# Group softmax over 285 MB: VectorE and ScalarE run hardware loops of 12 rows with semaphores of their own

## The chip, the cores and the metric

One core of a Trainium2 chip. The time is the device time of one execution in microseconds (us). The profile is one execution taken by the hardware profiler; its span, from the first to the last instruction, is about 2 us shorter than the time.

## The reference, cut to what matters

```python
B, N, D, G = 4, 4096, 4352, 8            # x: float32
x_g = x.reshape(B, N, G, D // G)         # groups of 544
x_g = x_g - x_g.max(axis=-1, keepdims=True)
exp = np.exp(x_g)
out = exp / exp.sum(axis=-1, keepdims=True)
```

285.21 MB are read and as much is written; each element is reduced, exponentiated and scaled once.

## The kernel before

A buffer holds 128 partitions of two rows (4.46 MB). SyncE (SP) issues 64 loads and 64 stores. For each row VectorE (DVE) takes the eight maxima, ScalarE (ACT) does eight exponentials that also sum, and VectorE multiplies eight times by the reciprocal. Everything is unrolled in Python, and a framework puts in the waits.

```python
pool = ctx.enter_context(tc.tile_pool(name="io", bufs=NBUF))       # NBUF = 6, R = 2
...
def expo(i, r):
    nc.vector.reduce_max(out=mx, in_=xr, axis=mybir.AxisListType.X, negate=True)
    for g in range(G):
        nc.scalar.activation(out=xr[:, g, :], in_=xr[:, g, :], func=Exp,
                             bias=mx[:, g:g + 1], scale=1.0, accum_out=sm[:, g:g + 1])

def scale(i, r):
    nc.vector.reciprocal(out=rs, in_=sums.pop((i, r)))
    for g in range(G):
        nc.vector.tensor_scalar_mul(out=xr[:, g, :], in0=xr[:, g, :], scalar1=rs[:, g:g + 1])
...
for n in range(len(work) + 1):           # work: 128 rows of 128 partitions
    if n < len(work):
        expo(*work[n])
    if n:
        i, r = work[n - 1]
        scale(i, r)
        if r == spans[i][1] - 1:
            store(i)
            if i + AHEAD < nt:           # AHEAD = 5
                load(i + AHEAD)
```

(Cuts are marked with "...", names shortened.)

## Time and profile before

| | before |
|---|---|
| time, median of the first 3 runs (lowest to highest) | 1335.78 us (1335.38 to 1341.09) |
| time and span of the profiled run | 1335.33 and 1333.5 us |
| first DMA issued, last part of the last store landed | 0.73 and 1332.6 us |
| instruction packets while the kernel ran | 28 |

The chain that ended last, followed back from the last instruction, by engine and then by line:

```profile
DMA 92%; DVE 4%; ACT 1%; SPq 1%; issue 0%; DVEq 0%; ACTq 0%
```

92% of the chain is data movement. The page's share of DMA is a mean over 16 DMA engines, though, and the last store lands over a stretch of 12.2 us (1320.4 to 1332.6), 0.9 us before the end: the kernel ends with the slowest of the 16. I call one DMA engine's work a **lane**. In the trace each transfer lands in 16 parts (2048 landing records for 128 transfers); the **lag** of a lane is how much later its part lands than the earliest part of the same transfer.

### The profile page before, as it was taken

Reading aid. Unit: us, or ns where it says so; the run is one execution under the profiler, and the core shown is the slowest. Engines: PE = TensorE matmul, PEld = TensorE weight load, DVE = VectorE, ACT = ScalarE, POOL = GpSimd, SP = SyncE. Lnnn points to the kernel's source line nnn. Section 1 sums busy time; section 2 is a strip of 40 time slices with the busy share of each in tenths; the row PEclk is TensorE's granted clock in tenths of the full one; section 3 lists DMA queues with packets and bytes.
Section 4 is the critical chain, followed back from the end, with each engine's and each line's share of the span. In section 5 each row is a group of like instructions: output and inputs, shape, how many; then the busy total and the mean of one; then the engine's idle time right before and its main releaser. Section 6 shows DMA issues by size and latency. Waiting matters only on the chain.

```text
span 1333.5 us, 3809 instructions
## 1 busy us (share of the span) xinstructions
DVE 1041.7 (78%) x1280; ACT 764.4 (57%) x2049; POOL 0.2 (0%) x4
## 2 busy tenths in 40 slices
DVE  5999887787877878778778787787877878778771
ACT  4777665555655556555565565655656556555560
POOL 0000000000000000000000000000000000000000
DMA  9999999999999999999999999999999999999996
GB/s 403 428 423 432 432 432 431 433 432 431 432 432 434 434 432 434 430 434 434 434 431 433 434 434 434 431 432 435 432 434 432 431 434 434 433 435 433 433 433 283
DMA packets 18460, 570.66 MB, mean 428 GB/s; under 512 B 2048, under 2 KB 2048, under 8 KB 2048
## 3 DMA queue, kind: packets, MB, share of 16 engines
q1 hardware_dynamic: 18432, 570.43, 99.3%
q14 instruction: 28, 0.23, 0.0%
HBM read 285.21 MB, written 285.21 MB: 428 GB/s over the span
## 4 chain that ended last, share of the span: by engine, by line
DMA 92%; DVE 4%; ACT 1%; SPq 1%; issue 0%; DVEq 0%; ACTq 0%
DMA out_dram<-xt 89%; DMA xt<-in_x_dram 3%; DVE mx L58 2%; DVE xt L76 1%; ACT xt L62 1%; SPq L47 1%; DVE rs L74 0%; DVEq L121 0%; ACTq L121 0%; ACTq L62 0%; SPq L50 0%
## 5 line engine op out<-in xcount | busy, mean ns | idle before, releaser
L62 ACT ACTIVATE xt<-xt,mx 128x544 f32<-128x544 f32 x1024 | 751.3, 735 | 522.0 <-DVE mx L58 504.4
L58 DVE TENSOR_REDUCE mx<-xt 128x8 f32<-128x4352 f32 x128 | 599.3, 4683 | 253.5 <-DMA xt<-in_x_dram 253.5
L76 DVE TENSOR_SCALAR xt<-xt,rs 128x544 f32<-128x544 f32 x1024 | 434.3, 499 | 4.5
L62 ACT ACTIVATION_READ_ACCUMULATOR xt<-xt,mx 128x1 f32 x1024 | 191.4, 187 | 0.0
L74 DVE RECIPROCAL rs<-sm 128x8 f32<-128x8 f32 x128 | 24.9, 194 | 4.0 <-ACT xt L62 4.0
L62 ACT ACT_TABLE_LOAD x1 | 1.3, 1283 | 13.7 <-DMA xt<-in_x_dram 13.7
L110 POOL MEMSET const-bfloat16-1.0<- 128x1 bf16 x1 | 0.1, 101 | 0.0
L110 POOL MEMSET const-uint8-127<- 128x1 uint8 x1 | 0.1, 101 | 0.0
L110 POOL MEMSET const-float32-0.0<- 128x1 f32 x1 | 0.1, 98 | 0.2 <-issue 0.2
L110 POOL MEMSET const-float32-1.0<- 128x1 f32 x1 | 0.1, 98 | 0.0
## 6 DMA issues: line engine op xcount, KB each, us to landing
xt<-in_x_dram SPq DMA_DIRECT2D x64, 4352.0 KB, 30.8
out_dram<-xt SPq DMA_DIRECT2D x64, 4352.0 KB, 40.7
```

Of the source, the lines that this page charges most:

```text
L47: nc.sync.dma_start(out=xt[:, :spans[i][1] * D], in_=rows(xf, i))
L58: nc.vector.reduce_max(out=mx, in_=xr, axis=mybir.AxisListType.X, negate=True)
L62: nc.scalar.activation(out=xr[:, g, :], in_=xr[:, g, :], func=mybir.ActivationFunctionType.Exp, bias=mx[:, g:g + 1], scale=1.0, accum_out= ...
L74: nc.vector.reciprocal(out=rs, in_=sums.pop((i, r)))
L76: nc.vector.tensor_scalar_mul(out=xr[:, g, :], in0=xr[:, g, :], scalar1=rs[:, g:g + 1])
L110: nc = _bacc.Bacc("TRN2", target_bir_lowering=False, num_devices=1)
```

## The change

Intent: keep the same work and the same DMAs, but let VectorE and ScalarE run a short loop in place of an unrolled stream. Buffers are fixed, so a loop body covers the 12 rows of the six buffers. A wait compares with a constant and counts the semaphore down at once, so that each turn finds the same values.

```diff
-    pool = ctx.enter_context(tc.tile_pool(name="io", bufs=NBUF))
+    ctx.enter_context(tc.tile_critical(no_gpsimd_drain=True))
+    ctx.enter_context(nc.cleanup_on_exit())
+    bufs = [ctx.enter_context(nc.sbuf_tensor(f"xt{b}", [P, R * D], f32)) for b in range(NT)]
+    landed = [nc.alloc_semaphore(f"landed{b}") for b in range(NT)]
+    stored = [nc.alloc_semaphore(f"stored{b}") for b in range(NT)]
...
+    def vector_max(s):
+        if s % R == 0:
+            nc.vector.sem_inc(landed[s // R], -16).wait_op(landed[s // R], 16, "sem-ge")
+        nc.vector.reduce_max(out=mx[:, s, :], in_=row(s), axis=X, negate=True).then_inc(max_done, 1)
+    def vector_scale(s):
+        nc.vector.sem_inc(exp_done, -1).wait_op(exp_done, 1, "sem-ge")
+        nc.vector.reciprocal(out=rs[:, s, :], in_=sm[:, s, :]).then_inc(rec_done, 1)
+        nc.vector.sem_inc(rec_done, -1).wait_op(rec_done, 1, "sem-ge")
...
+    def loop(engine):
+        return nc.Fori(
+            0, turns, engines=OrderedEngineSet([engine.engine]), head_slot={engine.engine: 0})
...
+        def _(vector):
+            vector_max(0)
+            with loop(vector):                          # S = 12 rows, turns = 10
+                for s in range(S):
+                    vector_max((s + 1) % S)
+                    vector_scale(s)
+            for n in range(turns * S, nr):              # the last 8 rows
+                if n + 1 < nr:
+                    vector_max((n + 1) % S)
+                vector_scale(n % S)
...
+        def _(scalar):
+            scalar.preload_act_table(Exp)
+            with loop(scalar):
+                for s in range(S):
+                    scalar_exp(s)
+            for n in range(turns * S, nr):
+                scalar_exp(n % S)
```

SyncE's part stays unrolled: five loads ahead, then for each buffer a wait for its two scaled rows, the store, a wait for the store of the buffer that comes free, and the next load.

## The prediction

> **What bounds the kernel now.** I read the page's busy shares first, then its DMA lines, the waits, one steady stretch of VectorE's timeline, and last the stages at the end of the run.

> ```profile
> DVE 1041.7 (78%) x1280; ACT 764.4 (57%) x2049; POOL 0.2 (0%) x4
> ...
> DMA packets 18460, 570.66 MB, mean 428 GB/s; under 512 B 2048, under 2 KB 2048, under 8 KB 2048
> ...
> q1 hardware_dynamic: 18432, 570.43, 99.3%
> q14 instruction: 28, 0.23, 0.0%
> ```

> The data queue keeps the 16 DMA engines busy for 99.3% of the span; VectorE (DVE) has 22% to spare and ScalarE (ACT) 43%. The change moves the same 570.43 MB. On that reading alone it is worth nothing. The last line matters later: 28 packets, 0.23 MB, were instructions, fetched by the same DMA engines.

> The view of waits, first for the engines, then for SyncE's queue:

> ```profile
> ACT xt L62 <- DVE mx L58: 504.4, 119, 7.5
> DVE mx L58 <- DMA xt<-in_x_dram: 253.5, 56, 13.7
> ...
> SPq L47 <- DMA out_dram<-xt: 1145.0, 58, 20.7
> SPq L50 <- DVE xt L76: 91.2, 7, 22.5
> ```

> The numbers are microseconds in total, times, and the longest. ScalarE waits for VectorE, VectorE for loads, and SyncE for stores to leave a buffer. Only 91.2 us of SyncE's waiting is for VectorE. The timeline of VectorE in the steady state shows its slack:

> ```profile
> 598.10 4.69 DVE L58 TENSOR_REDUCE mx<-xt 128x8 f32<-128x4352 f32 x1 [4.21 <-DMA xt<-in_x_dram]
> 602.70 0.19 DVE L74 RECIPROCAL rs<-sm 128x8 f32<-128x8 f32 x1
> 602.93 3.39 DVE L76 TENSOR_SCALAR xt<-xt,rs 128x544 f32<-128x544 f32 x8
> ...
> 618.64 4.68 DVE L58 TENSOR_REDUCE mx<-xt 128x8 f32<-128x4352 f32 x1 [4.20 <-DMA xt<-in_x_dram]
> ```

> One buffer (two rows) takes 618.64 - 598.10 = 20.54 us, of which VectorE idles 4.20. A store lands 40.7 us after its issue (median of the page's list of issues), and a 4.46 MB transfer takes 10.3 us at 433 GB/s, so some three transfers, 30 us, wait in the queues at any time. A compute delay below that starves no DMA engine.

> The end of the run is where something can be won:

> ```profile
> 600.00:1200.00 600.00, 471.37 (x581) 345.83 (x928) 0.00 (x0) 1.00 1.00 433
> ...
> 1315.00:1320.00 5.00, 0.00 (x0) 0.00 (x0) 0.00 (x0) 1.00 0.97 418
> 1320.00:1325.00 5.00, 0.00 (x0) 0.00 (x0) 0.00 (x0) 1.00 0.29 125
> 1325.00:1330.00 5.00, 0.00 (x0) 0.00 (x0) 0.00 (x0) 1.00 0.13 56
> 1330.00:1333.50 3.50, 0.00 (x0) 0.00 (x0) 0.00 (x0) 1.00 0.05 20
> ```

> The last two columns are DMA share and GB/s. From 1325 to 1330 the share is 0.13, and 2/16 is 0.125: fourteen DMA engines are done, two still work. The trace's landing records (each transfer lands in 16 parts, one per DMA engine) say the same: the parts of the first load land within 0.7 us, those of the last store from 1320.4 to 1332.6 us. Two parts lag by 12.2 and 11.8 us, the next four by 4.8, 4.4, 3.4 and 3.0, and ten by at most 0.7. The two lags grow in steps during the whole run, at the times of instruction packets. By the spacing of the packets, 10 belong to VectorE's stream, 17 to ScalarE's and 1 to SyncE's, one for each 128 or so recorded instructions. Around a packet the lane loses, for VectorE, 0.31 us for the packet and 0.58 us more because the data packet after it takes 1.87 us instead of 1.29; for ScalarE 0.31 + 0.31. So 10 x 0.89 = 8.9 us of the first lag and 17 x 0.62 = 10.5 us of the second are instruction fetch. The kernel ends with its slowest DMA engine.

> [...]

> **The change, part by part.** (1) The loops. The program holds 152 VectorE instructions in the loop and 99 after it; ScalarE has 110 and 73, where each of the 96 and 64 activations leaves a second, accumulator-reading record as it does now, so 206 and 137. [...] If they stay resident over their 10 turns, about 3 fetches are left for VectorE and 4 for ScalarE (my estimate from 251 and 343 instructions in 128-instruction packets, with one beyond). VectorE's lane then lags 12.2 - 8.9 + 3 x 0.89 = 6.0 us, ScalarE's 11.8 - 10.5 + 4 x 0.62 = 3.8, and the lane at 4.8, which fell back early in the run and hardly grows after 400 us, stays. The last landing comes 12.2 - 6.0 = 6.2 us earlier: **-6.2**. (2) Own semaphores. Each row gets separate counting-down waits: two on VectorE (two and a half with the load's), one on ScalarE. At 0.1 to 0.2 us each (an estimate from the 0.23 us that now lie between the starts of reciprocal and first multiply) VectorE's buffer grows by at most 1 us, against 4.20 idle: **0**. (3) Back edges: 10 on each engine, off the path as long as one costs less than the 4.20 us that VectorE idles in each buffer: **0**. (4) SyncE: the same 128 DMAs in the same order, each wait now inside its DMA: **0**. (5) The activation table is loaded at the start instead of at 13.70 us; the first reduction (13.65 to 18.35) covered it: **0**. (6) Frame: a hand-over and two branches before the first DMA, two more barriers after the last landing. Now 0.9 us pass from the last landing to the end with two barriers in it; I add **+1.0** there and **+0.3** in front. Sum: 1335.8 - 6.2 + 1.3 = 1330.9.

> **The rivals.** First, that bodies do not stay resident: [...] With one fetch a turn VectorE's lane lags 3.3 + 13 x 0.89 = 14.9 us, 1340 to 1341 in all with the frame; with two, 3.3 + 23 x 0.89 = 23.8, so 1349. Against it: the chosen slot is evidence that somebody looked. I give it 0.3. Second, that the fetch lag was hidden anyway, or that another lane takes its place: then 1335 to 1337. Against it stands the 0.13 above. Third, that new waits make VectorE the bound. It would take 4.20 us a buffer, or 2.1 us a row; a row's waits would have to cost ten times what they seem to. Then each further microsecond a row is 128 us, a loss over 2%. I give it 0.02.

> **Range and chances.** The resident case puts the end between 1328 and 1334, depending on how far the early lags, which look like chance, differ. The first rival stretches the upper side to 1345. The floor is the fast lanes' end, 1320.4 + 0.9 + 2.3 (time less span) = 1323.6 before any frame cost, so 2% (26.7 us) faster is out of reach. Predicted 1331, range 1327 to 1345; faster 0.01, same 0.97, slower 0.02.

> **What would show it.** Instruction packets falling from 28 to about 8 to 12; in the stages of the last 15 us, the stretch at two sixteenths shrinking from about 8 us to 2 or so; the last landings' spread at 5 to 6 us; steady rate still 433 GB/s; VectorE still idle 3 us or more a buffer. More than 40 packets would show the first rival, a steady rate below 430 the third. A first DMA issue later than 1.5 us, or over 3 us from last landing to end, would show that I mis-sized the frame.

(The "one beyond" in the 3 and 4 packets is an allowance of mine that no trace had shown. The chosen slot is `head_slot` in the edit above. The first rival: its packets per turn, one or two, were my estimate.)

## The result, and the profile after

The changed kernel took 1331.13 us (median of 4 runs, 1330.5 to 1332.2), the kernel before 1336.51 in the same comparison (4 runs). The ratio is 0.9954, 95% interval 0.993 to 0.9979. (Ratios here and below are the mean time of one kernel's fast runs over that of the other's of the same rounds, so not quite the ratio of the medians.) That is "same" by the 2% rule and yet a real gain of 0.5%.

The page of the changed kernel, busy shares and queues:

```profile
DVE 1041.5 (78%) x1280; ACT 764.4 (58%) x2049; POOL 0.2 (0%) x4
...
DMA packets 18441, 570.51 MB, mean 429 GB/s; under 512 B 2048, under 2 KB 2048, under 8 KB 2048
...
q1 hardware_dynamic: 18432, 570.43, 99.6%
q14 instruction: 9, 0.07, 0.0%
```

The engines' work is unchanged to 0.2 us, the data too. Of 28 instruction packets 9 are left. Its chain view has only VectorE's last instructions (`DVE 0%; DVEq 0%; issue 0%`): the waits are now separate instructions, and the view loses the chain there. That is no new bound, as the waits show, again in us in total, times, and the longest:

```profile
ACT xt L72 <- ACTq L69: 528.7, 127, 17.2
DVE mx L56 <- DVEq L55: 233.1, 56, 14.6
...
SPq L96 <- DMA out_dram<-xt: 1141.2, 58, 20.7
SPq L102 <- DVE xt L64: 102.4, 6, 33.3
```

They are the old waits under new names: L69 and L55 are the counting-down waits for the maxima and for the load. SyncE still waits 1141 us for stores and 102 for VectorE. VectorE's timeline in the steady state:

```profile
596.25 4.69 DVE L56 TENSOR_REDUCE mx<-xt 128x8 f32<-128x4352 f32 x1 [3.98 <-DVEq L55]
600.85 0.19 DVE L60 RECIPROCAL rs<-sm 128x8 f32<-128x8 f32 x1
601.20 3.39 DVE L64 TENSOR_SCALAR xt<-xt,rs 128x544 f32<-128x544 f32 x8
...
616.82 4.68 DVE L56 TENSOR_REDUCE mx<-xt 128x8 f32<-128x4352 f32 x1 [3.99 <-DVEq L55]
```

A buffer takes 616.82 - 596.25 = 20.57 us, as before. From the start of the reciprocal to the first multiply there are now 0.35 us in place of 0.23: the price of the separate wait, and VectorE's idle time per buffer falls from 4.20 to 3.99 us. It costs nothing, because loads set the pace: VectorE waits 233.1 us for them, and the rate below is still 433 GB/s. The stages at the end (DMA share and GB/s in the last two columns):

```profile
600.00:1200.00 600.00, 475.54 (x588) 348.31 (x935) 0.00 (x0) 1.00 1.00 433
...
1315.00:1320.00 5.00, 0.00 (x0) 0.00 (x0) 0.00 (x0) 1.00 0.92 397
1320.00:1325.00 5.00, 0.00 (x0) 0.00 (x0) 0.00 (x0) 1.00 0.26 111
1325.00:1328.70 3.70, 0.00 (x0) 0.00 (x0) 0.00 (x0) 1.00 0.01 2
```

The steady rate is the same 433 GB/s. The five microseconds at two sixteenths, 1325 to 1330, are gone. From the landing records of the last store: its earliest part lands at 1320.4 us before and 1320.3 after, its last part at 1332.6 before and 1326.2 after. So the fast lanes did not change at all, and the slow ones gained 6.4 us.

The records of DMA packets do not name lanes, but they can be told apart: on a lane each packet starts 3 or 4 ns before the one before it ends. Followed that way, all instruction packets of one engine lie on one lane. In the kernel before, VectorE's 10 are on the lane that ends last, ScalarE's 17 on the second, SyncE's on a third; in the changed kernel VectorE's 3 (at 18.4, 24.4 and 110.7 us) are again on the lane that ends last. (Where two lanes end within a few ns of each other the following can swap them, so it is used below only where it is clear.)

From the last landing to the end 0.9 us passed before and 2.5 us now. In spans: 1333.5 - 6.4 + 1.6 = 1328.7, which is the measured span.

### The profile page after: what moved, and what is told of

It is laid out like the page before. It is cut to its first block, busy times and chain, and to the rows that moved or that the text cites. A ratio compares the mean times of both kernels' runs of the same rounds, so it can differ in the third digit from the quotient of the medians.

```text
span 1328.7 us, 4036 instructions
## 1 busy us (share of the span) xinstructions
DVE 1041.5 (78%) x1280; ACT 764.4 (58%) x2049; POOL 0.2 (0%) x4
## 2 busy tenths in 40 slices
DMA packets 18441, 570.51 MB, mean 429 GB/s; under 512 B 2048, under 2 KB 2048, under 8 KB 2048
## 3 DMA queue, kind: packets, MB, share of 16 engines
q1 hardware_dynamic: 18432, 570.43, 99.6%
## 5 line engine op out<-in xcount | busy, mean ns | idle before, releaser
L56 DVE TENSOR_REDUCE mx<-xt 128x8 f32<-128x4352 f32 x128 | 599.1, 4680 | 234.0 <-DVEq L55 233.1
## 6 DMA issues: line engine op xcount, KB each, us to landing
xt<-in_x_dram SPq DMA_DIRECT2D x64, 4352.0 KB, 30.8
out_dram<-xt SPq DMA_DIRECT2D x64, 4352.0 KB, 40.7
```

The costliest lines, as they stand in the source:

```text
L56: nc.vector.reduce_max(out=mx[:, s, :], in_=row(s), axis=X, negate=True).then_inc(max_done, 1)
```

## The experiments

My theory: the end is set by the slowest lane, and a lane falls back by each instruction packet that it carries (in the trace of the kernel before by about 0.89 us for one of VectorE's and 0.62 for one of ScalarE's). The rivals: the own semaphores and the shorter list of waits give the gain; each packet or each loop is worth a share of its own; the packets are bystanders. Eleven kernels ran, all correct, in three groups, each group on one chip with its own runs of the kernel before. The times:

| run | time, median (runs) | ratio to before (95%) | packets, page | last store: earliest part, lag of the slowest two lanes, us |
|---|---|---|---|---|
| before | 1335.78 (3) | | 28 | 1320.4, 12.2, 11.8 |
| changed | 1331.13 (4) | 0.9954 (0.993 to 0.9979) | 9 | 1320.3, 5.9, 5.8 |
| e1_unrolled | 1339.0 (5) | 1.0022 (1.0009 to 1.0035) | 31 | 1320.4, 14.6, 13.8 |
| e2_only_vector_loops | 1338.16 (6) | 1.0026 (1.0012 to 1.0039) | 22 | 1320.2, 13.4, 6.5 |
| e3_only_scalar_loops | 1338.36 (5) | 1.0019 (1.0006 to 1.0032) | 18 | 1320.2, 17.0, 7.7 |
| e4_24_rows | 1353.17 (4) | 1.0135 (1.0121 to 1.015) | 32 | 1325.9, 16.7, 3.0 |
| e5_pool_3072 | 1375.94 (6) | 1.029 (1.0262 to 1.0318) | 33 | 1353.9, 16.8, 1.5 |
| e6_pool_1024 | 1331.39 (6) | 0.9956 (0.993 to 0.9982) | 17 | 1320.2, 7.1, 6.1 |
| e7_pool_loop | 1334.84 (6) | 0.9983 (0.9957 to 1.0009) | 10 | 1320.2, 10.3, 5.7 |
| e8_no_slot | 1331.05 (6) | 0.9953 (0.9927 to 0.9979) | 6 | 1320.4, 6.5, 5.7 |
| e9_pool_paced | 1340.93 (5) | 1.0037 (1.0023 to 1.0051) | 33 | 1320.4, 16.9, 10.2 |
| e10_short_end | 1331.0 (5) | 0.9967 (0.9954 to 0.9981) | 8 | 1320.3, 6.6, 6.4 |
| after_again | 1330.77 (5) | 0.9963 (0.9949 to 0.9977) | 9 | 1320.2, 5.6, 5.1 |

In each row but e4 and e5 the fast lanes end at 1320.2 to 1320.4 us, and the span is that number plus the largest lag plus the 0.9 (before) or 1.9 to 2.5 us of the frame's end.

### e1_unrolled: both loops undone

```diff
-            with loop(vector):
-                for s in range(S):
-                    vector_max((s + 1) % S)
-                    vector_scale(s)
-            for n in range(turns * S, nr):
+            for n in range(nr):
...
-            with loop(scalar):
-                for s in range(S):
-                    scalar_exp(s)
-            for n in range(turns * S, nr):
+            for n in range(nr):
                 scalar_exp(n % S)
```

> Both loops of the changed kernel are unrolled again; own semaphores, order, frame and DMAs stay. Fetch theory (the end is set by the DMA lane that fetched most instructions): about 1600 VectorE and 2180 ScalarE instructions, so 12 and 17 packets come back; VectorE's lane lags 3.3 + 12 x 0.89 = 14 us, and 1320.3 + 14 + 2.5 (last landing to end) + 1.8 (time less span) = 1338 to 1339: slower than the kernel before, because the longer frame stays. Rival (the gain comes from the own semaphores and the folded waits): 1331, as the changed kernel.

1339.0 us. The page's queue line of this kernel, and its last stages:

```profile
q14 instruction: 31, 0.25, 0.0%
```

```profile
600.00:1200.00 600.00, 471.39 (x580) 345.86 (x928) 0.00 (x0) 1.00 1.00 433
1320.00:1325.00 5.00, 0.00 (x0) 0.00 (x0) 0.00 (x0) 1.00 0.36 153
1325.00:1330.00 5.00, 0.00 (x0) 0.00 (x0) 0.00 (x0) 1.00 0.13 56
1330.00:1335.00 5.00, 0.00 (x0) 0.00 (x0) 0.00 (x0) 1.00 0.08 35
```

The packets are back, the share of two sixteenths is back, and the steady rate is still 433. The gain is wholly the loops'; the semaphores alone, with their longer frame and their wait instructions (13 packets of VectorE in place of 10), make the kernel 0.2% slower than before. The slowest lag, 14.6 us, is VectorE's and meets the 14 that the sum of packets gave; ScalarE's 13.8 is 2 us over the 11.7 that the same sum gives it. The rival of the semaphores is dead.

### e2 and e3: one loop each

```diff
# e2: ScalarE unrolled as in e1, VectorE's loop kept
# e3: VectorE unrolled as in e1, ScalarE's loop kept
```

> Only VectorE keeps its loop; ScalarE is unrolled. Fetch theory with the slowest lane deciding: ScalarE's lane lags 1.2 + 17 x 0.62 = 11.7 us, VectorE's about 6: 1336 to 1337, no gain over the kernel before. Rival (each loop saves a share of its own): half of the way between the changed kernel and the fully unrolled one, about 1334 to 1335. Rival (semaphores): 1331.

> Only ScalarE keeps its loop; VectorE is unrolled. Fetch theory with the slowest lane deciding: VectorE's lane lags 3.3 + 12 x 0.89 = 14 us: 1338 to 1339, the same as with both unrolled. Rival (each loop saves a share): about 1334 to 1335. Rival (semaphores): 1331.

1338.16 and 1338.36 us: either loop alone brings nothing, and both together 8 us. A rival in which each loop saves a share is out. The lag column says why: in each run one lane is as far back as in e1 (13.4, 17.0) and the other has recovered (6.5, 7.7). e2 came out a little over its 1336 to 1337; the lag of 13.4 is 1.7 over the expected 11.7. In e3 the profiled run (1341.22 us, above the median) has a lag of 17.0, more than the packets' sum; it grew from 11.9 at 1001 us by 5.1, with three packets on that lane in that time, 2.7 us. So 2.4 us came without packets, in steps, from a lag of about 12 on; e5 below shows such a creep more clearly. It is no rule: e1's slowest lane stood at 13.9 to 14.0 from 1197 to 1290 us.

### e4_24_rows: a longer body

```diff
-    turns = (nr - 1) // S
+    L = 2 * S
+    turns = (nr - 1) // L
...                                     # loops over range(L), slots s % S
```

> Loops of 24 rows and 5 turns in place of 12 rows and 10 turns: bodies of 304 and about 412 instructions[...]. [...] 3 packets a turn for VectorE (16 in all), 4 for ScalarE (21): VectorE's lane lags 3.3 + 16 x 0.89 = 17.5, 1342. [...] the packets stay near 10 and the time near 1331.

(The first case, to 1342, is bodies that are fetched again in each turn; the second, at 1331, bodies that are not.)

```profile
q14 instruction: 32, 0.26, 0.0%
```

32 packets, and 1353.17 us (the profile is of the quickest of the four runs, 1346.64). By lanes, 26 packets are ScalarE's, 5 VectorE's and 1 SyncE's. ScalarE's come five a turn, around its branch (at 220.3 us, with packets at 214, 224 and 229) and later in the body (306 and 388), and so in each of the four turns that follow a branch back. VectorE has none between 202 and 1308 us, over four of its branches back. So the body of 412 instructions is fetched again in each turn and the body of 304 is not. Neither case of the expectation came true: it had 16 packets for VectorE and 21 for ScalarE, or about 10 in all. The lane that ends last is ScalarE's, not VectorE's; the direction of the time was right for another reason, and the size was not (1342). The lag reached 15.0 us at 1000 us and 19.4 at 1200; from then on the fast lanes fell behind too (1325.9 against 1320.3), which is the state that e5 is in for most of its run.

### e5, e6, e7: packets without work

The idle GpSimd executes instructions that touch no data and that nobody waits for.

```diff
+        @block.gpsimd
+        def _(gpsimd):
+            for n in range(3072):                          # e6: range(1024)
+                gpsimd.sem_inc(idle, -1 if n % 2 else 1)
# e7: the same 3072 as a loop of 96 over 32 turns
```

> The changed kernel, and the idle GpSimd runs 3072 unrolled instructions that only raise and lower an own semaphore: no data, no wait, nobody waits for them. They need 24 instruction packets more. Fetch theory: some lane falls back by 24 x 0.62 to 0.89 us = 15 to 21 us and ends last: 1340 to 1346. Rival (fetch is a bystander, 0.2 MB in 570 MB): the time stays at 1331.

> The same with 1024 instructions, 8 packets. Fetch theory with the slowest lane deciding: a lane that falls back by 8 x 0.62 to 0.89 = 5.0 to 7.1 us, where others lag 5.9 anyway: 1330 to 1332.5, next to nothing, if the lane is clean; up to 1338 if it is one of those that lag. A rival in which every packet costs its share of the time: a third of the loss of the 3072.

> Control: the same 3072 instructions executed as a loop of 96 over 32 turns. As many instructions, semaphore updates and as much sequencer work, but 2 or 3 packets. Fetch theory: 1331. Rival (the instructions themselves disturb, for instance the semaphores): the loss of the unrolled 3072.

e5 took 1375.94 us. 24 more packets of 8192 bytes, 0.2 MB beside 570, cost 45 us. That settles that packets are no bystanders, and misses my 1340 to 1346 by far. The windows of e5 show where the rest went:

```profile
100.00:260.00 160.00, 130.17 (x161) 95.40 (x257) 0.00 (x0) 1.00 1.00 432
260.00:400.00 140.00, 109.17 (x138) 83.47 (x224) 0.00 (x0) 1.00 1.00 432
400.00:500.00 100.00, 78.30 (x93) 54.08 (x145) 0.00 (x0) 1.00 1.00 424
500.00:600.00 100.00, 75.23 (x96) 55.59 (x151) 0.00 (x0) 1.00 1.00 418
600.00:700.00 100.00, 74.71 (x94) 57.29 (x154) 0.00 (x0) 1.00 1.00 420
700.00:900.00 200.00, 154.71 (x191) 111.13 (x299) 0.00 (x0) 1.00 1.00 419
900.00:1100.00 200.00, 153.28 (x188) 111.91 (x301) 0.00 (x0) 1.00 1.00 416
```

All GpSimd packets fall before 250 us, when the rate is still 432; the loss comes after 400 us, with no packet of GpSimd, at 416 to 424 GB/s. In the landing records the slow lane lags 15.2 us at 261 us, as far as 24 packets of 0.6 us take it. Then it creeps to 18 to 19 without any, stays there, and from then on all lanes are slow: two transfers take 21.3 us in place of 20.57. At the end the fast lanes are 33.6 us later than in the changed kernel (1353.9 against 1320.3), and the slowest lags 10.9 us more. The DMA share still reads 1.00, because the data packets take longer (1.333 us in the mean from 600 to 1200 us, against 1.288) and count as busy all that time: the GB/s column shows the loss, the share doesn't. My estimate for the limit of 18 to 19, which no run tests: SyncE waits for a store before it issues the next pair (1177.4 us in 58 waits here); a load lands 30.8 us after its issue in the changed kernel and a transfer takes 10.3, half of the 20.57, so about two transfers (20.5 us) are then still queued on the slowest lane, and a lane that is further ahead than these would have nothing to do. A lag of 17.0 us, in e3, still left the fast lanes at 1320.2. Why the slowest lane itself goes slower in that state stays open.

e6 took 1331.39 us, no more than the changed kernel: 8 packets more on a lane that had room cost nothing, where a third of e5's loss would be 15 us. In these runs the end is a maximum over lanes, not a sum.

e7 was expected at 1331 and took 1334.84, in six runs between 1334.78 and 1335.26. It has 10 packets, so the instructions as such are not what cost 45 us; but it is 3.5 us too slow. In its landing records the slowest lane lags 5.6 us at 261 us and then drifts to 10.3 in small steps, about 0.075 us for each buffer. It is the lane on which SyncE's only packet (at 757 us) shows as a step of 0.8. The same drift is in the changed kernel (from 0.7 at 261 to 5.3) and in the kernel before; there it starts on a lane that had not fallen back early. Here it does. What decides which lanes fall back in the first 260 us (by 5.3, 4.4, 3.3 and 2.5 us in the changed kernel, packets counted) stays open.

### e8_no_slot: the placement

```diff
-            0, turns, engines=OrderedEngineSet([engine.engine]), head_slot={engine.engine: 0})
+            0, turns, engines=OrderedEngineSet([engine.engine]))
```

> The changed kernel without the placement of the loops' heads[...]. [...] fetched again in each turn: 2 packets a turn, 1345 to 1349. [...] nothing changes: 1331.

(The two cases are bodies that are fetched again, with two packets a turn by my estimate of 128 instructions to a packet, and bodies that are not.)

1331.05 us and 6 packets, three fewer than with the placement. The placement is worth nothing here: bodies of 152 and 206 instructions are not fetched again without it, in 10 turns, nor with it (9 packets). Together with e4, which has the placement: 304 is not fetched again either (5 packets for VectorE), 412 is (26 for ScalarE).

### e9_pool_paced: the same packets, spread out

```diff
             for n in range(3072):
-                gpsimd.sem_inc(idle, -1 if n % 2 else 1)
+                i = gpsimd.sem_inc(idle, -1 if n % 2 else 1)
+                if n % 24 == 0:
+                    i.wait_op(scaled, n // 24 + 1, "sem-ge")
```

> The 3072 unrolled GpSimd instructions again, but 24 of them for each row that VectorE has scaled, so that the 24 extra packets are spread over the whole run in place of the first 250 us. Unrolled at once they cost 45 us where the sum of the packets was 15 to 21: in that trace the lane had fallen back 15 us by 260 us, then crept on to 18 to 19 without packets, and from there all lanes slowed down (433 to 417 GB/s) for the rest of the run. Theory (the packets cost their sum; the rest came from the long time with a lag near 18 us): the lag grows evenly to 1 + 24 x 0.62 = 16 us plus some creep at the end, 1341 to 1346. Rival (an unrolled packet costs 45/24 = 1.9 us wherever it falls): 1376 again.

```profile
1310.00:1315.00 5.00, 0.00 (x0) 0.00 (x0) 0.00 (x0) 1.00 0.97 418
1315.00:1320.00 5.00, 0.00 (x0) 0.00 (x0) 0.00 (x0) 1.00 0.98 425
1320.00:1325.00 5.00, 0.00 (x0) 0.00 (x0) 0.00 (x0) 1.00 0.29 125
1325.00:1330.00 5.00, 0.00 (x0) 0.00 (x0) 0.00 (x0) 1.00 0.11 49
1330.00:1335.00 5.00, 0.00 (x0) 0.00 (x0) 0.00 (x0) 1.00 0.06 28
```

1340.93 us, at the foot of the expected range, against 1375.94 for the same 33 packets at the start. The fast lanes end at 1320.4, one lane (1/16 is 0.06) works on alone until 1337. So the packets cost their sum, about 10 us over the changed kernel, and the other 35 us of e5 come from when the packets fall. That it is the long time with a lag near 18 us is argued, not shown alone: e4 and e5 both lose their rate at a lag of 18 to 20 us.

### e10_short_end and after_again: a better version?

```diff
-    ctx.enter_context(nc.cleanup_on_exit())
...
-                sync.wait_ge(stored[b], 16 * ((nt - b + NT - 1) // NT))
+                n = 16 * ((nt - b + NT - 1) // NT)
+                sync.sem_inc(stored[b], -n).wait_op(stored[b], n, "sem-ge")   # and the same for scaled
```

> The changed kernel with a shorter end: SyncE counts its own semaphores down to zero in its last waits, so that the clearing of the semaphores and the barrier after it can go. The last landing stays at 1326 us; from it to the end 2.5 us become about 2.0: 1330.6, 0.5 us under the changed kernel, which is less than the interval against the kernel before can show and has to be seen in the spans.

> The changed kernel itself, on the same chip as the other two, for their comparison: 1331.

1331.0 and 1330.77 us. The end got shorter as expected (1.9 us from the last landing to the end, against 2.5), but its slowest lane lagged 6.6 us against 5.6, and the time did not fall. I have no version that beats the changed kernel.

## Why the prediction was right

The time was predicted at 1331 and measured at 1331.13. By its own steps:

- **What bounds the kernel.** Shown. The fast lanes end at 1320.3 us with or without the loops, and e1, e2, e3, e6 and e9 move the end with the slowest lane alone.
- **The loops, -6.2.** The last landing moved by -6.4. The number of packets was right (9 on the page, predicted 8 to 12; 3 + 4 from the two engines, SyncE's one, and one at 1328.6 us, after the last landing). The lag of 6.0 was right (5.9), and it is VectorE's: its three packets lie on the lane that ends last, here and in after_again, and 5.9 - 3 x 0.89 = 3.2 us of other lag is what the prediction had (3.3). ScalarE's lane was mis-sized: it stands at 5.8 where 3.8 was predicted, with the four packets expected, because its other lag is 3.3 us and not 1.3. The drift of SyncE's lane, now at 5.3, was not foreseen, and the lane at 4.8 has no counterpart (the next is at 4.0). That neither of the two others ended last is luck: 0.2 us more on ScalarE's lane would have done it, and in e10 it does end last.
- **Own semaphores, 0.** Right: 0.21 us of VectorE's idle time in each buffer, where up to 1 had been allowed.
- **Back edges, 0.** Right. The branch itself takes 56 ns on VectorE and 45 on ScalarE (medians), and the next instruction of the loop is not late: across VectorE's branch at 116.8 us the reduction starts 3.31 us after the first multiply, and 3.30 in the row before, which has no branch.
- **SyncE and the table, 0.** Nothing contradicts it: the table's load is now at 0.90 us, and the first reduction starts when its load has landed, as before.
- **The frame, +1.3.** Mis-sized: 0.22 in front (0.73 to 0.95 us for the first DMA) and 1.6 behind, 1.8 in all. Only the 1.6 adds to the -6.4, which is measured from the start of the span: -4.8, where -4.9 was predicted.
- **The rivals.** The first, bodies that don't stay resident, is false for 12 rows (9 packets with the placement, 6 without), and true for 24 in ScalarE's body of 412 instructions alone (26 of e4's 32 packets). The second, a lane taking the place of the ones relieved, is true to a part: VectorE's lane still ends last at 5.9 us, and ScalarE's (5.8) and SyncE's (5.3) are close behind it. The third, VectorE as the bound, is false.
- **"Early lags, which look like chance."** Probably false: e7 repeats its 1334.8 within 0.5 us six times, as if the early lags went with the program; only one of the six has a profile, so that is not shown.
